# A decoder layer on one Trainium2 core: which queue loads the first projection weights, and how the convolution's state is loaded and turned

## The chip, the core and the metric

The kernel runs on one core of one Trainium2 chip. The core's engines work side by side, each through its own instructions in order: TensorE (PE in the profile; its weight loads are PEld), VectorE (DVE), ScalarE (ACT), GpSimd (POOL) and SyncE (SP), which here only issues transfers. ScalarE and GpSimd can issue transfers too. The metric is the device time of one execution in microseconds (us), the median of several runs.

## What is computed

One layer for a prompt of 1024 tokens and for 8 sequences of 8 new tokens, all in fp32. The reference, cut to what matters here:

```python
def layer_forward(h, p, pos, gla_s0, conv_prev, attend, lw):
    u = rmsnorm(h, lw['g_mix']) @ lw['w_in']
    ...                                  # gated linear attention -> o_gla, latent attention -> o_mla
    h = h + jnp.concatenate([o_gla, o_mla], axis=-1) @ lw['w_o']
    y, conv_new = conv_ffn(rmsnorm(h, lw['g_ffn']), conv_prev, lw)
    h = h + y
    h = h + (p @ lw['ple_w_proj']) * jax.nn.sigmoid(rmsnorm(h, lw['g_ple']) @ lw['ple_w_gate'])

def conv_ffn(n, prev, lw):
    a, c = n @ lw['ffn_w_gate'], n @ lw['ffn_w_up']
    full = jnp.concatenate([prev, a], axis=1)              # prev: state_conv, 2 rows per sequence
    conv = lw['ffn_conv_b'] + sum(lw['ffn_conv_w'][j] * full[:, j:j + T] for j in range(3))
    return (jax.nn.silu(conv) * c) @ lw['ffn_w_down'], full[:, -2:]
```

The model width is 1024, the inner width of the gated network 2816 (22 groups of 128). The new tokens attend to a paged cache of 8192 positions for each sequence.

## The kernel before

A float32 product is made of three matmuls. `split` writes an operand's rounded part with a cast (ScalarE, L115, names ending in h) and the remainder with a subtraction (VectorE or GpSimd, L116, names ending in l); a product is then high by high, high by low and low by high.

The longest stage streams the cache: for each block, pages are turned on TensorE (`ctp`, L522), split into `cTh` and `cTl`, multiplied into keys (`ks`, L139 to L141), squared and summed for the norm (`csq` on ScalarE, L560; `css` on VectorE, L565), scaled by `ca` and `cy` (L586 to L590), scored (`csr` from `kTh`, `kTl`; `sn`, L592 and L594 on GpSimd), reduced to a maximum (`ml`, L598), turned (`mt`, L616) and multiplied with the latents (`cpv`, L645, summed into `pvs`, L653). Beside it runs dense work for the prompt in small units that a generator hands out: from about 1060 us the output projection with w_o, `wo_units`. Each `wo_unit` is six matmuls into one PSUM bank, `ps_dn` (L1432, L1435, L1436), and one add on VectorE into the residual `h` (L1439). There are three groups of two row blocks c of w_o, each with two column halves f, and a fourth group for the end.

A projection operand is loaded into a buffer tagged "stage", of which there are three, and then split: `oraw` from the intermediate `doT` (`wo_rows`, L1409, into `sh`, `sl`) and `wraw` from w_o (`wo_cols`, L1417, into `wdh`, `wdl`). At the entry (g = 0, q = 0) SP issues, in the code's order, two oraw, two wraw for half 0, x blocks h0 to h3 (L1550, 128 x 1024 words each), two wraw for half 1, two oraw, h4 to h7 and `hs` (L1555). The first oraw and wraw blocks, up to `wraw_14736`, were loaded earlier.

At the end of the first group `conv_state` loads the convolution's weights (66 rows) and bias (22 rows) into the stage tile `cvec` (L1481, L1482), turns them on TensorE into `pt_cv` (L1484) and copies them to `convT` on ScalarE (L1486). Three more turns take 128, 128 and 96 rows of state_conv through stage tiles `sc` (L1492) and banks `pt_sc` (L1494) to `prev` (L1495). The banks pt_cv, pt_sc and ps_dn come from one pool of three. Another buffer in the same pool as the stage tiles, tagged "fd", is used by `fold_sample` (L1454 to L1456), which adds the new tokens' part of the projection into hs; between the first group's fold and the next there is a long pause.

In the last group each finished residual row block is taken up by `normed` (L1588): its squares are summed on ScalarE (L1465), its rows are stored as `dhp` by a transfer that ScalarE issues (L1592), and it is scaled in place, on VectorE in most cases (L1474). The scaling of a block in place waits for the landing of its store.

The order of each engine's instructions is not that of the code alone. The kernel is built inside a context that places instructions by a simulated timeline; the code's order and priorities are its input, and some matmuls are held where they stand. So a small edit can move other instructions.

## Time and profile before

| what | value |
|---|---|
| median of 3 runs | 2216.89 us (2215.88 to 2218.55) |
| the profiled execution | 2221.39 us |
| its span, first to last instruction | 2219.6 us |
| mean granted TensorE clock | 0.984 |
| TensorE busy | 2134.6 us (96%) |
| VectorE busy | 1666.6 us (75%) |
| ScalarE busy | 1369.1 us (62%) |
| GpSimd busy | 1227.5 us (55%) |

In the profile `L115` is line 115 of the kernel, `wdh<-wraw` means output from input without buffer numbers, and a bracket such as `[2.06 <-ACT wdh L115]` gives the idle time of the engine just before the instruction and what ended it. A group's time runs from the start of its first to the end of its last instruction. A window row gives each engine's busy time in a stretch, and the clock that TensorE was granted in it, 1.00 being full speed. The chain of waits follows the end of the program back through whatever released each step. PEq, SPq and ACTq are an engine's issuing of instructions and transfers.

### The profile page before, as it was taken

What the parts mean: (1) busy time and instruction counts of PE and PEld (TensorE: products, weight loads), DVE (VectorE), ACT (ScalarE), POOL (GpSimd) and SP (SyncE); (2) the same over time, 40 slices, a digit from 0 to 9 for tenths busy, and PEclk for the clock granted to TensorE, in tenths of its full rate; (3) what the DMA queues carried; (4) which work ended last, traced back from release to release, by engine and by line L of the source; (5) the groups of instructions that cost most, each with busy time, mean ns of one, the idle gap of its engine ahead of it and who ended that gap; (6) DMA issues with size and microseconds to landing.
All of it is one profiled execution on the core that took longest, in us unless ns stands there. A gap on an engine that the chain in (4) does not pass through costs nothing.

```text
span 2219.6 us, 38384 instructions
## 1 busy us (share of the span) xinstructions
PE 2134.6 (96%) x13460; PEld 1934.7 (87%) x13460; DVE 1666.6 (75%) x2551; ACT 1369.1 (62%) x3726; POOL 1227.5 (55%) x1330
## 2 busy tenths in 40 slices
PE   7999999999999999999999987999999999999999
PEld 6888978878888888887788876999999999888899
DVE  4775676467788888887888878888888886887642
ACT  5576766777778888887777766433333433534631
POOL 5675668576777777777445557666656562011100
PEclk9899999999999999999999998999999999999999
DMA  5343234412342222221521212322232325778321
GB/s 181 110 141 110 77 117 157 141 54 69 104 120 60 64 73 61 60 56 46 167 80 57 76 66 96 105 92 95 91 100 91 100 87 190 238 222 237 98 72 41
DMA packets 204418, 233.07 MB, mean 105 GB/s; under 512 B 42422, under 2 KB 146339, under 8 KB 204227
## 3 DMA queue, kind: packets, MB, share of 16 engines
q1 hardware_dynamic: 188259, 179.49, 25.8%
q0 software_dynamic: 14736, 46.67, 7.3%
q10 hardware_dynamic: 1232, 4.46, 0.5%
q8 instruction: 108, 1.77, 0.3%
q14 instruction: 83, 0.68, 0.1%
HBM read 188.00 MB, written 42.52 MB: 104 GB/s over the span
## 4 chain that ended last, share of the span: by engine, by line
PE 80%; DVE 7%; ACT 5%; DMA 4%; POOL 2%; issue 2%; SPq 0%; DVEq 0%; POOLq 0%; ACTq 0%
PE ps_gu L140 7%; PE ps_gu L141 7%; PE ps_gu L139 7%; PE ks L139 5%; PE ks L141 5%; PE ks L140 4%; PE ps_dn L141 3%; PE ps_dn L140 3%; PE ps_dn L139 3%; PE cpv L645 2%; PE ctp L522 2%; PE ps_lt L278 2%; PE ps_pj L139 2%; PE ps_pj L140 1%; PE ps_pj L141 1%
## 5 line engine op out<-in xcount | busy, mean ns | idle before, releaser
L560 ACT ACTIVATE csq<-ks 128x256 f32<-128x256 f32 x1040 | 392.2, 400 | 88.1 <-PE ks L141 78.0
L565 DVE TENSOR_REDUCE css<-csq 128x16 f32<-128x1024 f32 (+1 forms) x264 | 315.8, 1197 | 63.0 <-ACT csq L560 61.9
L115 ACT CAST wh<-st 128x512 fp32r<-128x512 f32 x176 | 108.4, 619 | 188.6 <-PE ps_gu L140 166.0
L139 PE MATMUL ks<-mv0h,cTh 128*128 128x320 f32 (+1 forms) x520 | 171.9, 333 | 6.9 <-ACT csq L560 3.0
L139 PE MATMUL ks<-mv1h,cTh 128*128 128x320 f32 (+1 forms) x520 | 170.4, 329 | 7.6 <-ACT sn L562 3.6
L604 POOL TENSOR_TENSOR chl<-craw,chl 128x1024 fp32r<-128x1024 f32 x64 | 141.8, 2216 | 57.9 <-ACT chl L603 57.2
L140 PE MATMUL ks<-mv1l,cTh 128*128 128x320 f32 (+1 forms) x520 | 154.0, 298 | 0.0
L140 PE MATMUL ks<-mv0l,cTh 128*128 128x320 f32 (+1 forms) x520 | 153.0, 296 | 0.0
L141 PE MATMUL ks<-mv0h,cTl 128*128 128x320 f32 (+1 forms) x520 | 148.6, 298 | 0.9 <-DVE cTl L116 0.8
L141 PE MATMUL ks<-mv1h,cTl 128*128 128x320 f32 (+1 forms) x520 | 148.9, 300 | 0.0
L630 POOL TENSOR_TENSOR phl<-sn,phl 128x512 fp32r<-128x512 f32 (+1 forms) x64 | 84.8, 1326 | 108.2 <-ACT phl L629 107.9
L116 DVE TENSOR_TENSOR wl<-st,wh 128x512 fp32r<-128x512 f32 x132 | 119.0, 903 | 28.5 <-ACT wh L115 28.5
L116 POOL TENSOR_TENSOR wl<-st,wh 128x512 fp32r<-128x512 f32 x44 | 69.4, 1580 | 103.5 <-ACT wh L115 98.2
L141 PE MATMUL ps_dn<-o 128*128 128x512 f32 x308 | 120.2, 390 | 0.0
L140 PE MATMUL ps_dn<-o 128*128 128x512 f32 x308 | 120.1, 390 | 0.1
L116 DVE TENSOR_TENSOR cTl<-ctp,cTh 128x512 fp32r<-128x512 f32 (+1 forms) x136 | 90.1, 663 | 39.4 <-ACT cTh L115 38.4
L139 PEld LDWEIGHTS ks<-mv0h,cTh 128*128 128x128 f32 x520 | 99.1, 191 | 20.7 <-ACT sn L562 7.1
L562 ACT COPY sn<-ks 128x64 f32<-128x64 f32 x520 | 116.8, 225 | 0.0
L139 PEld LDWEIGHTS ks<-mv1h,cTh 128*128 128x128 f32 x520 | 99.6, 191 | 19.7 <-ACT sn L562 7.4
L1317 POOL TENSOR_TENSOR pl<-p,ph 128x512 fp32r<-128x512 f32 (+1 forms) x96 | 97.1, 1016 | 31.7 <-DVE ph L1316 21.5
L139 PE MATMUL ps_dn<-o 128*128 128x512 f32 x308 | 112.1, 390 | 0.0
L139 PE MATMUL ps_gu<-xrh,wh 128*128 128x320 f32 x352 | 108.6, 309 | 1.1 <-ACT xrh L115 1.1
(672 smaller groups left out, 7875.3 us busy)
## 6 DMA issues: line engine op xcount, KB each, us to landing
raw<-ds SPq DMA_DIRECT2D x77, 256.0 KB
raw<-ffn_w_down SPq DMA_DIRECT2D x66, 256.0 KB
stage<-w_in SPq DMA_DIRECT2D x48, 256.0 KB
st<-ffn_w_gate SPq DMA_DIRECT2D x44, 256.0 KB
st<-ffn_w_up SPq DMA_DIRECT2D x44, 256.0 KB
wr<-ffn_w_down SPq DMA_DIRECT2D x44, 256.0 KB
ds<-cv SPq DMA_DIRECT2D x21, 512.0 KB
oraw<-doT SPq DMA_DIRECT2D x16, 256.0 KB
```

What stands on the lines that cost most here:

```text
L115: cast = act.copy(hi, src)
L116: res = (lo_eng or dve).tensor_tensor(lo, src, hi.bitcast(F32), ALU.subtract)
L139: pe.matmul(ps, ah, bh, start=first, stop=False)
L140: pe.matmul(ps, ah, bl, start=False, stop=False)
L141: return pe.matmul(ps, al, bh, start=False, stop=last)
L278: pe.matmul(ps, x, w, start=first, stop=last)
L560: act.activation(sq[:, f * 256:f * 256 + 256], ks[:, 0:256], AF.Square)
L562: act.copy(o.sn[:, g0 + i, :], ks[:, 256:320])
L565: dve.tensor_reduce(o.ss[:, g0 + i + 1 - n:g0 + i + 1, :].rearrange("p i h -> p (i h)"), sq2[:, :n].rearrange("p i (h n) -> p (i h) n", n= ...
L604: pool.tensor_tensor(ch[:, c0:c1, 128:256], src, ch[:, c0:c1, 0:128].bitcast(F32), ALU.subtract)
L630: pool.tensor_tensor(phl[:, :nt, 64:128], sb, phl[:, :nt, 0:64].bitcast(F32), ALU.subtract)
L1317: pool.tensor_tensor(pl[:, c0:], p[:, c0:], ph[:, c0:].bitcast(F32), ALU.subtract)
```

## The change

Two edits are made.

The first gives `wo_cols` an argument for the issuing queue. At the entry the first block of w_o for half 0 still goes through SP; the second block and both blocks of half 1 go through ScalarE's queue. The order in which the code names the loads stays the same.

The second loads everything that `conv_state` turns into one tile `cs` of 128 x 4 x 128 words in the "fd" buffer: three pieces of state_conv, and the convolution's weights and bias in the fourth column block. Four turns write 128, 128, 96 and 88 columns of one bank, and two copies on ScalarE take 352 columns to `prev` and 88 to `convT`, where there were four copies. The number of loads (five) and of turns (four) is as before.

```diff
-    def wo_cols(c, f):
+    def wo_cols(c, f, ring=sp):
...
-        sp.dma_start(raw, A["w_o"][0][c * P:(c + 1) * P, f * 512:f * 512 + 512])
+        ring.dma_start(raw, A["w_o"][0][c * P:(c + 1) * P, f * 512:f * 512 + 512])
...
     def conv_state():
-        cvec = stage([88, P], F32, "cvec")
-        sp.dma_start(cvec[0:66], A["ffn_conv_w"][0].rearrange("j (f p) -> (j f) p", p=P))
-        sp.dma_start(cvec[66:88], A["ffn_conv_b"][0].rearrange("(f p) -> f p", p=P))
+        cs = fold_tile([P, 4, P], F32, "cs")
+        scv = A["state_conv"][0].rearrange("b j (f p) -> (b j f) p", p=P)
+        parts = [(c, min(P, 352 - c * P)) for c in range(3)] + [(3, 88)]
+        for c, n in parts[:3]:
+            sp.dma_start(cs[:n, c], scv[c * P:c * P + n])
+        sp.dma_start(cs[0:66, 3], A["ffn_conv_w"][0].rearrange("j (f p) -> (j f) p", p=P))
+        sp.dma_start(cs[66:88, 3], A["ffn_conv_b"][0].rearrange("(f p) -> f p", p=P))
         pt = pd([P, 512], "pt_cv")
-        pe.transpose(pt[:, 0:88], cvec, ident[:88, :88])
+        for c, n in parts:
+            c0 = min(c * P, 352)
+            pe.transpose(pt[:, c0:c0 + n], cs[:n, c], ident[:n, :n])
         convT = z["convT"] = z["fx"].tile([P, 88], F32, name="convT")
-        act.copy(convT, pt[:, 0:88])
         prev = z["fx"].tile([P, 352], F32, name="prev")
-        scv = A["state_conv"][0].rearrange("b j (f p) -> (b j f) p", p=P)
-        for c0 in range(0, 352, P):
-            n = min(P, 352 - c0)
-            sc = stage([P, P], F32, "sc")
-            sp.dma_start(sc[:n], scv[c0:c0 + n])
-            pt = pd([P, 512], "pt_sc")
-            pe.transpose(pt[:, 0:n], sc[:n], ident[:n, :n])
-            act.copy(prev[:, c0:c0 + n], pt[:, 0:n])
+        act.copy(prev, pt[:, 0:352])
+        act.copy(convT, pt[:, 352:440])
...
-                    for ld, x in ((wo_rows, 0), (wo_cols, 0)):
-                        for c in grp:
-                            ld(c, x)
+                    for c in grp:
+                        wo_rows(c, 0)
+                    for c, ring in zip(grp, (sp, act)):
+                        wo_cols(c, 0, ring)
                     for t in range(NT):
                         sp.dma_start(hrows(t), A["x_prompt"][0, t * P:(t + 1) * P, :])
                         if t == 3:
-                            for ld, x in ((wo_cols, 1), (wo_rows, 1)):
-                                for c in grp:
-                                    ld(c, x)
+                            for c in grp:
+                                wo_cols(c, 1, act)
+                            for c in grp:
+                                wo_rows(c, 1)
```

The order of instructions differs from the entry of the projection (about 1060 us) to about 1282 us on all engines, is the same again to about 1318, and has small swaps from there to about 1390. The counts of matmuls are the same; ScalarE has two copies fewer and three transfers more, SP three transfers fewer.

At the entry, ScalarE's order (`-` before, `+` after; the number behind a name tells buffers apart) takes up the three transfers among the squares of one cache block:

```order
 L115 CAST cTh_15065<-ctp_15060 128x512
 L560 ACTIVATE csq_15011<-ks_15029 128x256
+L1417 DMA wraw_14742<-w_o 128x512
 L588 ACTIVATE ca_15047<-cy_15046 128x64
+L1417 DMA wraw_14752<-w_o 128x512
+L1417 DMA wraw_14758<-w_o 128x512
 L560 ACTIVATE csq_15080<-ks_15081 128x256
 L562 COPY sn_14985<-ks_15081 128x64
```

On SP, `wraw_14742` stood behind the fourth x block and the other two behind the fifth; now x blocks follow one another there. At the same place VectorE's order changes:

```order
 L565 TENSOR_REDUCE css_14986<-csq_15011 128x16
 L589 SCALAR_TENSOR_TENSOR ca_15047<-css_14802,ca_15047 128x64
+L590 SCALAR_TENSOR_TENSOR cy_15046<-ca_15047,cy_15046 128x64
 L565 TENSOR_REDUCE css_14986<-csq_15080 128x16
-L590 SCALAR_TENSOR_TENSOR cy_15046<-ca_15047,cy_15046 128x64
+L598 TENSOR_REDUCE ml_15055<-sn_14801 128x64
 L116 TENSOR_TENSOR wdl_14741<-wraw_14742,wdh_14740 128x512
-L598 TENSOR_REDUCE ml_15055<-sn_14801 128x64
+L622 TENSOR_SCALAR mt_15174,bm_15176<-mt_15174,bm_14965 128x128
 L1439 TENSOR_TENSOR h0_14699<-h0_14699,ps_dn_15104 128x512
```

The operation cy moved ahead of a css, and the maximum ml moved ahead of the remainder wdl of the second w_o block.

At the convolution's state, TensorE's order before, from the last keys of one block on:

```order
L141 MATMUL ks_16110<-mv0h_98,cTl_15846 128x256
L139 MATMUL csr_16216<-qbd0h_102,kTh_16212 128x256
L140 MATMUL csr_16216<-qbd0l_103,kTh_16212 128x256
L1484 MATMUL pt_cv_16143<-ident_61,cvec_16140 128x88
L141 MATMUL csr_16216<-qbd0h_102,kTl_16213 128x256
L139 MATMUL csr_16216<-qbd0h_102,kTh_16212 128x256
L140 MATMUL csr_16216<-qbd0l_103,kTh_16212 128x256
L141 MATMUL csr_16216<-qbd0h_102,kTl_16213 128x256
L1494 MATMUL pt_sc_16150<-ident_61,sc_16148 128x128
L1494 MATMUL pt_sc_16155<-ident_61,sc_16153 128x128
L1494 MATMUL pt_sc_16160<-ident_61,sc_16158 128x96
L1432 MATMUL ps_dn_16166<-wdh_15875,sh_15640 128x512
```

And after, the place to which the four turns moved:

```order
L1432 MATMUL ps_dn_16084<-wdh_14740,sh_14768 128x512
L1435 MATMUL ps_dn_16084<-wdl_14741,sh_14768 128x512
L1436 MATMUL ps_dn_16084<-wdh_14740,sl_14769 128x512
L1490 MATMUL pt_cv_16146<-ident_61,cs_16140 128x128 x2
L1490 MATMUL pt_cv_16146<-ident_61,cs_16140 128x96
L1490 MATMUL pt_cv_16146<-ident_61,cs_16140 128x88
L139 MATMUL ks_16093<-mv0h_98,cTh_15845 128x320
L140 MATMUL ks_16093<-mv0l_99,cTh_15845 128x320
```

The turns now stand a dozen units earlier, right behind the last ps_dn of a unit and ahead of the keys. The scores csr, which stood between the turns, follow only behind the next ps_dn (six matmuls), ctp (four) and two sets of ks (six). On ScalarE the copies to prev and convT moved ahead of the squares of this block, and the cast of `sh_16134` with the cast cTh after it. On SP the five loads stand ahead of two oraw and one wraw behind which they stood:

```order
 L1417 DMA wraw_16118<-w_o 128x512
+L1484 DMA cs_16140<-state_conv 128x128 x2
+L1484 DMA cs_16140<-state_conv 96x128
+L1485 DMA cs_16140<-ffn_conv_w 66x128
+L1486 DMA cs_16140<-ffn_conv_b 22x128
 L1409 DMA oraw_16124<-doT_84 128x512
 L1417 DMA wraw_16130<-w_o 128x512
 L1409 DMA oraw_16136<-doT_84 128x512
-L1481 DMA cvec_16140<-ffn_conv_w 66x128
-L1482 DMA cvec_16140<-ffn_conv_b 22x128
-L1492 DMA sc_16148<-state_conv 128x128
-L1492 DMA sc_16153<-state_conv 128x128
```

In the last group VectorE's scaling of h6 moved up. Before:

```order
L1439 TENSOR_TENSOR h6_14692<-h6_14692,ps_dn_18399 128x512
L1439 TENSOR_TENSOR h7_14693<-h7_14693,ps_dn_18415 128x512
L1439 TENSOR_TENSOR h7_14693<-h7_14693,ps_dn_18423 128x512
L653 SCALAR_TENSOR_TENSOR pvs_18448<-pvs_18291,mb_18397,cpv_18439 128x258
L1474 SCALAR_TENSOR_TENSOR h6_14692<-h6_14692,rs_14697,gb_14695 128x1024
L1439 TENSOR_TENSOR h0_14699<-h0_14699,ps_dn_18465 128x512
```

After:

```order
L1439 TENSOR_TENSOR h6_14692<-h6_14692,ps_dn_18391 128x512
L1439 TENSOR_TENSOR h7_14693<-h7_14693,ps_dn_18407 128x512
L1474 SCALAR_TENSOR_TENSOR h6_14692<-h6_14692,rs_14697,gb_14695 128x1024
L1439 TENSOR_TENSOR h7_14693<-h7_14693,ps_dn_18415 128x512
L653 SCALAR_TENSOR_TENSOR pvs_18440<-pvs_18283,mb_18389,cpv_18431 128x258
L1439 TENSOR_TENSOR h0_14699<-h0_14699,ps_dn_18457 128x512
```

The second add of h7 and pvs, which stood ahead of the scaling of h6, now stand behind it.

## The prediction

> **What bounds the kernel now.** I read the page first, then the chain of waits, then the windows of the two stretches that the change touches. The page gives the share of each engine in the chain that ended last:
>
> ```profile
> PE 80%; DVE 7%; ACT 5%; DMA 4%; POOL 2%; issue 2%; SPq 0%; DVEq 0%; POOLq 0%; ACTq 0%
> ```
>
> TensorE is the bound: 80% of the chain. So an edit is worth what it gives TensorE: idle time, or time at a lowered clock. The chain names both stretches by their transfers, w_o at the entry of the projection, then the convolution's loads (start, length, what):
>
> ```profile
> 1062.86 5.92 DMA wraw<-w_o
> ...
> 1069.46 1.32 DVE wdl L116
> ...
> 1145.13 1.90 DMA cvec<-ffn_conv_b
> ...
> 1151.01 0.43 PE ps_dn L1435
> ```
>
> The windows show what the second costs (columns: width, busy time of PE, PEld, DVE, ACT and POOL with counts, granted clock, DMA share, GB/s):
>
> ```profile
> 1144.00:1146.00 2.00, 1.26 (x11) 1.06 (x9) 1.73 (x4) 2.00 (x8) 0.81 (x1) 1.00 0.35 102
> 1146.00:1148.00 2.00, 1.34 (x8) 1.03 (x8) 1.73 (x2) 1.51 (x5) 1.98 (x2) 1.00 0.47 150
> 1148.00:1150.00 2.00, 0.47 (x2) 0.14 (x1) 2.00 (x4) 0.53 (x2) 0.57 (x2) 0.86 0.20 57
> 1150.00:1152.00 2.00, 1.86 (x5) 1.60 (x6) 0.33 (x1) 0.24 (x1) 1.76 (x2) 0.50 0.60 183
> 1152.00:1154.00 2.00, 2.00 (x8) 1.61 (x7) 0.69 (x1) 0.00 (x0) 1.78 (x2) 0.50 0.79 237
> 1154.00:1156.00 2.00, 2.00 (x10) 2.00 (x9) 1.34 (x2) 1.59 (x5) 0.00 (x0) 0.50 0.61 217
> 1156.00:1158.00 2.00, 2.00 (x11) 1.73 (x11) 1.19 (x2) 1.09 (x4) 0.23 (x1) 0.93 0.05 18
> 1160.00:1180.00 20.00, 20.00 (x130) 18.02 (x129) 15.34 (x23) 14.91 (x49) 8.84 (x8) 1.00 0.12 34
> ```
>
> Busy time by clock over the first seven rows is 1.26 + 1.34 + 0.40 + 0.93 + 1.00 + 1.00 + 1.86 = 7.8 us of work at full clock in 14 us: 6.2 us are lost, of which 3.1 are idle (14 less 10.93 busy) and 3.1 the half clock that follows. The last row says that a gain made here stays: behind it TensorE never waits for 20 us.
>
> By the Trainium skill, page "TensorE: Matmul & The Clock Gate", Part 1, the gate opens again after one busy window of about 3.4 us. Here the clock stays at 0.50 from 1150 to 1156 under unbroken work, over 6 us; by the page's window the half clock would cost about 1.7 us and not 3.1, and the sum below would be 1.4 us smaller. The measured rows decide.
>
> **The convolution's state: fewer waits.** The idle time has four pieces:
>
> ```profile
> 1146.29 0.39 PE L139 MATMUL csr<-qbd0h,kTh 128*128 128x256 f32 x1 [1.02 <-ACT kTh L115]
> 1147.16 0.27 PE L1484 MATMUL pt_cv<-ident,cvec 88*128 88x88 f32 x1 [0.37 <-DMA cvec<-ffn_conv_b]
> 1149.20 0.33 PE L1494 MATMUL pt_sc<-ident,sc 128*128 128x128 f32 x1 [1.06 <-DMA sc<-state_conv]
> 1150.14 0.39 PE L1494 MATMUL pt_sc<-ident,sc 96*128 96x96 f32 x1 [0.61 <-DMA sc<-state_conv]
> ```
>
> The last three are waits for loads, 2.04 us. The loads were late because their stage buffers were still held; the new tile takes the "fd" buffer, and SP has the five loads ahead of the next oraw. The last reader of that buffer ends here:
>
> ```profile
> 1115.83 0.67 DVE L1456 TENSOR_TENSOR hs<-hs,ps_ds 64x512 f32<-64x512 f32 x1
> ...
> 1146.75 0.62 ACT L115 CAST sh<-oraw 128x512 fp32r<-128x512 f32 x1
> 1148.18 0.27 ACT L1495 COPY prev<-pt_sc 128x128 f32<-128x128 f32 x1 [0.49 <-PE pt_sc L1494]
> 1154.04 0.58 ACT L115 CAST cTh<-ctp 128x512 fp32r<-128x512 f32 x1 [3.23 <-PE ctp L522]
> 1154.65 0.69 DVE L116 TENSOR_TENSOR cTl<-ctp,cTh 128x512 fp32r<-128x512 f32 x1 [0.78 <-ACT cTh L115]
> ```
>
> So the loads go out at about 1116.5, and with 1.90 us each they have long landed when their transposes come, near 1142. The five issues cost SP at most the same as before; no one waits for SP there. The 2.04 us go. The csr matmuls, for which kTh was awaited (1.02 us), now stand behind six ps_dn, four ctp and six ks matmuls, so that wait goes too.
>
> What is late next is ScalarE. It works without a gap up to 1147.4 (the end of the sh row), and still has the two new copies in front: the one of 352 columns I put at 0.45 us (0.27 for 128 columns in the row above, 0.62 for the 512 of sh; between these ends nearer the upper by its columns), the one of 88 as before, 0.23. Both stand ahead of sh now, so its end moves to about 1148.0, and the cast cTh after it ends at 1148.6. On VectorE sl (0.69, the length of cTl) stands ahead of cTl, which then ends at about 1149.6. TensorE has meanwhile run dry: it stood at about 1145.3 before the csr wait, has 0.44 us of transposes more by then, and then six ps_dn (0.43 at half clock in the chain, so 0.215 each, 1.3 in all) and ctp (0.4): about 1147.4. The first two ks need cTh alone (0.3 us), so it waits 1149.6 - 1147.4 - 0.3 = 1.9 us for the cast and the subtraction. The sum here is 6.2 - 1.9 = 4.3 us gained. The ends: 6.2, when nothing waits, and 2.04, when only the loads' waits go and the clock falls as before. VectorE would allow 5.0 (14 less its 9.0 us busy in the seven windows). Two copies fewer on ScalarE and no change in the transposes' columns: nothing more from these.
>
> **The entry's weights: ScalarE's queue.** Here TensorE stands from 1067.4 to 1070.8 but for one matmul:
>
> ```profile
> 1064.22 0.44 ACT L560 ACTIVATE csq<-ks 128x256 f32<-128x256 f32 x1
> 1066.30 1.22 DVE L565 TENSOR_REDUCE css<-csq 128x16 f32<-128x1024 f32 x1
> 1067.80 1.07 POOL L592 TENSOR_TENSOR sn<-sn,cy 128x512 f32<-128x512 f32 x1 [8.67 <-DVE cy L590]
> 1068.95 1.27 POOL L594 TENSOR_TENSOR sn<-sn,sr 128x512 f32<-128x512 f32 x1
> 1069.48 0.49 PE L1432 MATMUL ps_dn<-wdh,sh 128*128 128x512 f32 x1 [2.06 <-ACT wdh L115]
> 1070.69 1.04 DVE L598 TENSOR_REDUCE ml<-sn 128x64 f32<-128x512 f32 x1
> 1070.82 0.71 PE L1435 MATMUL ps_dn<-wdl,sh 128*128 128x512 f32 x1 [0.85 <-DVE wdl L116]
> ...
> 1068.00:1070.00 2.00, 0.49 (x1) 0.19 (x1) 0.54 (x1) 0.62 (x1) 1.92 (x2) 1.00 1.03 350
> 1070.00:1072.00 2.00, 1.18 (x3) 0.99 (x4) 1.74 (x3) 1.25 (x3) 0.42 (x2) 0.74 1.03 376
> 1072.00:1074.00 2.00, 2.00 (x10) 1.96 (x9) 1.89 (x3) 1.44 (x4) 0.04 (x1) 0.50 1.03 420
> ```
>
> The awaited block went out on SP at 1062.86, behind four x blocks, and landed at 1068.78. On ScalarE's queue it goes out behind the csq of 1064.22, so at about 1064.5, 1.6 us later. The DMA share is 1.03 with 350 to 420 GB/s: the engines are full, and moving the request makes no bytes fewer. If the two rings share the engines, a block of 256 KB has half of some 390 GB/s and takes 1.3 us, with the 1.90 us that the small cvec load took from issue to landing some 3.2 in all: it lands from 1067.7 on, and I allow up to 1068.8. If what was issued first is served first, it stands behind two more x blocks (h4 and h5, 128 x 1024 words each, 1.05 MB at 390 GB/s, 2.7 us) and lands at about 1071.5. I take the landing as unmoved, nearer the first.
>
> It then gives little, since VectorE's order changed: ml (L598) now stands ahead of the awaited wdl. The operation cy, for which POOL waits, is one place up and no longer stands behind the second css (1.22), so it is 1.2 us earlier: POOL's two operations end near 1069.0, ml near 1070.1, and wdl, 0.69 as the cTl of its size took, near 1070.9 instead of 1070.77 (1.32 in the chain's row, beside POOL). TensorE restarts at 1071.0 instead of 1070.8: +0.2 us. The ends: -3.0 (landing early, clock kept) and +2.7.
>
> **The drain.** At 1322 VectorE's order is changed in one more place, and with it some swaps up to 1365:
>
> ```profile
> 1318.76 1.87 DVE L1439 TENSOR_TENSOR h<-h,ps_dn 128x512 f32<-128x512 f32 x3
> 1320.98 0.33 ACTq L1592 DMA_DIRECT2D dhp<-h  x1
> 1322.25 1.29 DVE L1474 SCALAR_TENSOR_TENSOR h<-h,rs,gb 128x1024 f32<-128x1024 f32 x1 [0.97 <-DMA dhp<-h]
> 1340.00:1360.00 20.00, 14.06 (x80) 10.82 (x81) 18.57 (x27) 15.19 (x30) 17.98 (x15) 0.77 0.31 106
> ```
>
> The norm of h6 waits for the landing of dhp. It now stands ahead of the last of the three adds and of pvs, which wait with it: up to the 0.97 us on VectorE, which from 1340 on is the fullest engine (18.57 of 20). The swaps behind it may give as much back. I take 0, with ends of -1 and +1.
>
> The dhp row also prices **the three issues on ScalarE** at the entry: 0.33 us each, 1.0 in all; the csq behind them moves by up to that, inside the 2.06 us that TensorE waits there. Cover gone, it would cost the 1.0. SP, freed of three issues, sends h4 to h7 earlier; nobody waits for these.
>
> **The sum**: -4.3 + 0.2 + 0 = -4.1 us. The profiled execution is 2221.39 us (span 2219.6), 4.5 above the median of 2216.89; the sum is a difference, so from the median: 2212.8 us. A measurement here can tell 0.2%, 4.4 us, from no change, so the likeliest value lies just inside that.
>
> **Rivals.**
> 1. The clock falls again. The new wait of 1.9 us for cTh and cTl comes within a stretch already short of work. For it: at the entry 2.06 and 0.85 us of waiting were enough for 0.50. Against: 1.9 is a single, shorter gap. Half clock for 6 us costs the 3.1: -4.1 + 3.1 = -1.0, about 2215.9.
> 2. The entry gains: the rings share, the block lands at 1067.7 or before, ml does not hold wdl. TensorE's gap shrinks by some 2 us, and the loss by clock (0.31 + 1.00 us in the rows 1070 to 1074) mostly goes: -3 more, about 2209.6. The Trainium skill, "DMA: Bandwidth & Descriptors", section "Queues, rings and completion order", has each DMA engine alternate between rows of queues by packets, which is this rival; no run here shows it yet. The same page, "Issuing engines are not separate DMA queues", speaks against it: another issuing engine saves only the time to issue.
> 3. First come, first served: +2.7 at the entry instead of +0.2, about 2215.3.
> 4. Slower: ScalarE's blocks are served last, after all that SP has sent. Restart is landing plus 2.04 us (1070.82 less 1068.78), one for one. Eight x blocks (4.2 MB), and what follows, at 390 GB/s from 1061 reach to 1072 to 1076. With a landing at 1076.6 the restart is 7.8 later and the half clock, then 6 us long, costs some 1.7 more than now: 9.5 - 4.3 = +5.2, about 2222.1. The entry eats the conv place's gain from a landing near 1072 on, and past 1076 it is slower by over 0.2%.
> 5. It does not do what it says, the loads still late: excluded as far as row 1115.83 goes; only another wait of SP could hold them.
>
> **How the numbers follow.** Forecast 0.42, of which 0.24 falls below 2212.5; rival 1, 0.15; rival 2, 0.20; rival 3, 0.10; slower, rival 4 with reordered stretches (1160 to 1282) that open a wait like this one's, 0.13. Faster by over 0.2%: 0.24 + 0.20 = 0.44. Slower: 0.13. Same: 0.43. The range goes from the conv place's best end with the entry's (6.2 + 3.0 off, 2207.7) to the third rival with the drain's +1 and the conv place at its lower end (2215.3 + 1 + 2.3 = 2218.6). The forecast alone has 2211 to 2214.5.
>
> **What would show it.** Right: no DMA among what ends TensorE's waits at 1140 to 1160, the clock at 1.00 there, a wait for cTh or cTl of about 2 us, the loads into cs near 1116; at the entry wdh's cast still near 1068.8 and wdl behind ml. Wrong: a clock of 0.50 after 1149, a cast of wdh later than 1071 or before 1067.5, or a new gap of over 2 us between 1160 and 1282, where the order changed and I count nothing.

## The result, and the profile after

The changed kernel takes 2230.3 us in the median (2228.61 to 2233.31), the kernel before, run beside it, 2218.86. The ratio is 1.0056 with an interval of 1.0043 to 1.0068: 0.56% slower, where 2212.8 us were forecast. The profiled span grew from 2219.6 to 2228.9 us, by 9.3.

To see where, both traces were laid side by side at five marks that every kernel here has: the last transfer at line 1334 ahead of the projection (1059.16 us before), the 16th, 31st and 49th of VectorE's additions at L1439 (1142.85, 1216.31, 1313.02), and the 201st matmul into ps_gu (1408.00). The table is worked out from the start times of these instructions; each entry is what the stretch takes more than before, in us.

| kernel | ahead | entry, to the 16th add | convolution, to the 31st | to the 49th | drain, to ps_gu | difference of the spans |
|---|---|---|---|---|---|---|
| the change | +0.9 | **+8.1** | **-4.5** | 0.0 | **+4.8** | +9.3 |

So the convolution's place gained what was forecast, and both places that were put near zero lost. These are the windows of the entry, first of the changed kernel, then of the kernel before (width; busy time of PE, PEld, DVE, ACT and POOL with counts; granted clock, DMA share, GB/s):

```profile
1060.00:1080.00 20.00, 13.74 (x73) 10.91 (x71) 13.12 (x21) 11.55 (x38) 2.58 (x4) 0.91 0.95 307
1080.00:1100.00 20.00, 16.39 (x90) 14.20 (x91) 15.58 (x22) 12.59 (x41) 8.19 (x6) 0.91 0.30 101
```

```profile
1060.00:1080.00 20.00, 15.50 (x84) 13.02 (x84) 15.87 (x23) 14.96 (x49) 2.79 (x4) 0.91 1.01 339
1080.00:1100.00 20.00, 19.58 (x124) 17.07 (x123) 18.53 (x30) 14.22 (x47) 11.39 (x10) 1.00 0.22 70
```

TensorE idles 9.9 of the 40 us instead of 4.9, and the second window runs at 0.91 instead of 1.00, which is at most 1.8 us more. Most of the loss is idle time. The timeline of the changed kernel names its causes (start, length, instruction, and in brackets the idle time before it and what ended it):

```profile
1063.77 3.78 ACTq L1417 DMA_DIRECT2D wraw<-w_o  x1
1067.60 0.26 ACT L588 ACTIVATE ca<-cy 128x64 f32<-128x64 f32 x1 [2.05 <-issue]
1067.68 1.07 ACTq L1417 DMA_DIRECT2D wraw<-w_o  x2
1068.80 0.38 ACT L560 ACTIVATE csq<-ks 128x256 f32<-128x256 f32 x1 [0.94 <-DVE cy L590]
1069.34 0.41 PE L139 MATMUL ks<-mv0h,cTh 128*128 128x256 f32 x1 [3.02 <-ACT sn L562]
1073.39 0.62 ACT L115 CAST wdh<-wraw 128x512 fp32r<-128x512 f32 x1 [2.79 <-DMA wraw<-w_o]
1076.54 0.62 ACT L115 CAST wdh<-wraw 128x512 fp32r<-128x512 f32 x1 [2.04 <-DMA wraw<-w_o]
1094.13 0.38 PE L141 MATMUL csr<-qbd0h,kTl 128*128 128x256 f32 x1 [2.17 <-DVE kTl L116]
```

The first row is the surprise: to issue one 256-KB load holds ScalarE's queue for 3.78 us. What the engine had been given before still runs, but the activation ca behind the issue comes 2.05 us late (second row). Behind ca stand the two other issues, 1.07 us together (third), and only then the square csq (fourth) and the copy sn, for which TensorE waits 3.02 us (fifth). The awaited block is cast at 1073.39, 4.6 us after its old landing of 1068.78, or 3.7 us if the 0.9 us are taken off by which this execution was late ahead of the entry; ScalarE stands 2.79 us for it, and 2.04 for the next block (sixth and seventh). The last row is a later consequence, taken up at the end. A point for later: the second and third issues took 0.54 and 0.44 us, with 1.7 and 2.0 MB in flight on SP and the transfer engines as full (DMA share 1.00). Only the first was long.

At the convolution the windows of the changed kernel that answer to those of 1144 to 1158 before:

```profile
1152.00:1154.00 2.00, 1.69 (x14) 1.43 (x13) 2.00 (x3) 2.00 (x9) 1.10 (x1) 1.00 0.00 0
1154.00:1156.00 2.00, 2.00 (x15) 1.78 (x14) 1.44 (x4) 2.00 (x8) 1.09 (x2) 1.00 0.56 166
1156.00:1158.00 2.00, 2.00 (x17) 1.91 (x15) 2.00 (x1) 1.89 (x7) 2.00 (x1) 1.00 0.80 238
1158.00:1160.00 2.00, 1.72 (x12) 1.36 (x12) 2.00 (x5) 1.01 (x4) 0.77 (x2) 1.00 0.14 55
```

TensorE idles 0.6 us in eight, the clock stays at 1.00, and no load ends a wait. The loads' own rows and the waits that are left:

```profile
1124.16 1.28 SPq L1484 DMA_DIRECT2D cs<-state_conv  x3
1153.16 1.24 PE L645 MATMUL cpv<-chl,phl 128*128 128x258 f32 x8 [0.31 <-POOL phl L630]
1158.56 0.39 PE L141 MATMUL csr<-qbd0h,kTl 128*128 128x256 f32 x1 [0.28 <-DVE kTl L116]
```

In the drain the loss is made at two places. The first is where VectorE's order changed: the scaling of h6 now stands ahead of the second addition of h7. The changed kernel's rows, the scaling of h6, that addition, the store of h7 and the scaling of h7:

```profile
1326.83 1.28 DVE L1474 SCALAR_TENSOR_TENSOR h<-h,rs,gb 128x1024 f32<-128x1024 f32 x1 [0.44 <-DMA dhp<-h]
1328.03 0.68 DVE L1439 TENSOR_TENSOR h<-h,ps_dn 128x512 f32<-128x512 f32 x1
1328.85 0.33 ACTq L1593 DMA_DIRECT2D dhp<-h  x1
1332.54 1.28 DVE L1474 SCALAR_TENSOR_TENSOR h<-h,rs,gb 128x1024 f32<-128x1024 f32 x1 [0.88 <-POOL rs L1467]
```

Before, that addition was the last of the three at 1318.76, the store of h7 went out at 1320.98, and h7 was scaled here:

```profile
1324.92 1.76 DVE L1474 SCALAR_TENSOR_TENSOR h<-h,rs,gb 128x1024 f32<-128x1024 f32 x1
```

Counted from the start of the 49th addition, the store of h7 goes out after 11.3 us instead of 8.0, and h7 is scaled after 15.0 instead of 11.9. TensorE also runs at half clock there for 6.8 us (0.50 in 1320 to 1324), so that an addition waits 1.67 us for ps_dn; the two are not parted in this kernel. At VectorE's fifth scaling, the last but one, VectorE is 2.6 us behind (24.6 us after the 49th addition instead of 22.0).

The second place is the last scaling, that of h5, whose rows are here the last addition, the store and the scaling:

```profile
1349.02 0.67 DVE L1439 TENSOR_TENSOR h<-h,ps_dn 128x512 f32<-128x512 f32 x1
1349.83 0.33 ACTq L1593 DMA_DIRECT2D dhp<-h  x1
1353.71 2.40 DVE L1474 SCALAR_TENSOR_TENSOR h<-h,rs,gb 128x1024 f32<-128x1024 f32 x1 [1.58 <-DMA dhp<-h]
```

The kernel before had this at the same place:

```profile
1341.01 1.27 DVE L1439 TENSOR_TENSOR h<-h,ps_dn 128x512 f32<-128x512 f32 x2
1342.43 0.33 ACTq L1592 DMA_DIRECT2D dhp<-h  x1
1346.20 1.28 DVE L1474 SCALAR_TENSOR_TENSOR h<-h,rs,gb 128x1024 f32<-128x1024 f32 x1 [0.69 <-POOL rs L1467]
```

In both kernels the store goes out 0.14 to 0.15 us after the end of h5's last addition. That addition is 2.9 us late, and VectorE was 2.6 of them behind already. By the time VectorE came to scale h5 before, only POOL's rs was awaited; now the store is, for 1.58 us, and the scaling then takes 2.40 us and not 1.28, so that it ends 4.1 us late.

### The profile page after: what moved, and what is told of

Its sections match the earlier page's. It is cut to its first block, busy times and chain, and to the rows that moved or that the text cites. A ratio compares the mean times of both kernels' runs of the same rounds, so it can differ in the third digit from the quotient of the medians.

```text
span 2228.9 us, 38384 instructions
## 1 busy us (share of the span) xinstructions
PE 2137.7 (96%) x13460; PEld 1934.2 (87%) x13460; DVE 1671.7 (75%) x2551; ACT 1367.8 (61%) x3724; POOL 1228.8 (55%) x1330
## 4 chain that ended last, share of the span: by engine, by line
PE 44%; DVE 3%; POOL 2%; issue 1%; ACT 1%; DMA 1%; DVEq 0%; POOLq 0%; ACTq 0%
PE ps_gu L140 7%; PE ps_gu L141 7%; PE ps_gu L139 7%; PE ps_dn L141 3%; PE ps_dn L140 3%; PE ps_dn L139 3%; PE ps_pg L141 1%; PE ps_pg L140 1%; PE ps_pg L139 1%; PE ps_dn L1432 1%; PE ks L139 1%; PE ps_dn L1436 1%; PE ps_dn L1435 1%; PE ps_ds L1753 1%; PE ks L141 1%
## 5 line engine op out<-in xcount | busy, mean ns | idle before, releaser
L139 PE MATMUL ks<-mv0h,cTh 128*128 128x320 f32 (+1 forms) x520 | 171.7, 332 | 11.3 <-ACT sn L562 7.4
L592 POOL TENSOR_TENSOR sn<-sn,cy 128x512 f32<-128x512 f32 (+1 forms) x64 | 70.4, 1100 | 76.8 <-DVE cy L590 69.0
```

What stands on the lines that cost most here:

```text
L139: pe.matmul(ps, ah, bh, start=first, stop=False)
L592: pool.tensor_tensor(snv, snv, y[:, :nt].rearrange("p i h -> p (i h)").unsqueeze(2).broadcast_to([P, nt * 8, 8]), ALU.mult)
```

## The experiments

The kernels of one experiment differ from the change or from before by the lines shown. The table gives each one's median, the interval of its ratio to before (run beside it), and the stretches as above. The stretches are those of one profiled execution each, which need not be the median one: it lies 4.7 us below the median for the kernel with the convolution alone and the drain's order kept, 2.6 below for half 0, and 2.6 above for the last but one row.

| kernel | median us | ratio | ahead | entry | convolution | to the 49th | drain | spans |
|---|---|---|---|---|---|---|---|---|
| the change | 2230.30 | 1.0043 to 1.0068 | +0.9 | +8.1 | -4.5 | 0.0 | +4.8 | +9.3 |
| convolution alone | 2218.16 | 0.9981 to 1.0002 | -2.5 | -1.0 | -5.4 | 0.0 | +5.5 | -3.2 |
| ring alone | 2231.58 | 1.0044 to 1.0073 | +0.8 | +8.8 | +0.1 | 0.0 | +0.4 | +10.0 |
| half 0 on ScalarE | 2225.26 | 1.0013 to 1.0034 | -0.6 | +3.8 | -5.4 | -1.6 | +4.7 | +1.2 |
| half 1 on ScalarE | 2225.39 | 1.0016 to 1.0037 | -0.6 | +4.9 | -4.4 | 0.0 | +4.0 | +3.8 |
| weights first | 2219.13 | 0.9984 to 1.0006 | -1.4 | -0.8 | -5.4 | +0.1 | +4.1 | -2.3 |
| the same, half 0 on ScalarE | 2226.95 | 1.0012 to 1.0036 | +1.5 | +5.0 | -5.4 | -1.4 | +5.6 | +5.5 |
| convolution alone, drain's order kept | 2214.06 | 0.9961 to 0.9987 | -4.0 | -1.3 | -5.4 | -1.6 | +0.3 | -12.0 |
| x in halves | 2219.65 (one time) | | -1.8 | +0.2 | -5.4 | -1.3 | +5.3 | -1.9 |
| weights alone first | 2212.54 | 0.9958 to 0.9983 | -1.1 | -2.9 | -5.4 | +0.2 | +0.1 | -9.1 |
| the same, half 0 on ScalarE | 2214.82 | 0.9968 to 0.9988 | -1.6 | +0.9 | -5.4 | -0.3 | +2.5 | -4.0 |
| the change, drain's order kept | 2224.92 | 1.0009 to 1.0035 | +0.8 | +7.5 | -4.4 | 0.0 | +0.2 | +4.1 |

Ahead of the first mark all kernels are alike, so the +1.5 to -4.0 us there are how much one execution differs from another. Two kernels have before's order at the entry too, and read -1.0 and -1.3 there: so far single executions can be off. "Half 0" is the one block of the first half that the change moves to ScalarE, "half 1" the other two.

**Convolution alone.** From the change, with before's code at the entry.

```diff
-                    for c in grp:
-                        wo_rows(c, 0)
-                    for c, ring in zip(grp, (sp, act)):
-                        wo_cols(c, 0, ring)
+                    for ld, x in ((wo_rows, 0), (wo_cols, 0)):
+                        for c in grp:
+                            ld(c, x)
```

> Only the convolution's tile, all w_o blocks through SP. Every engine has the order of before up to the convolution and that of the change from there on. Theory A (the loss is made at the entry by ScalarE's queue, the convolution's place gives its 4.4 us, the drain's extra 4.7 us is an accident of the clock): no loss at the entry, -4 us in all, about 2214.5 us. Theory B (the new order at the drain costs 4.7 us in itself): -4.4 + 4.7, no change, about 2219. In both TensorE waits for no load between 1140 and 1160 us.

The convolution gives 5.4, and the drain takes 5.5 back: the ratio cannot be told from 1. The entry has nothing to do with the drain's loss. Nor does that loss need the half clock, for here TensorE's clock is 1.00 from 1304 to 1345, and what h6 costs stands by itself (its scaling, then the store of h7):

```profile
1313.36 2.99 DVE L1474 SCALAR_TENSOR_TENSOR h<-h,rs,gb 128x1024 f32<-128x1024 f32 x1 [2.22 <-DMA dhp<-h]
1317.09 0.33 ACTq L1591 DMA_DIRECT2D dhp<-h  x1
```

VectorE stands 2.22 us for the store of h6, where it stood 0.97 before, and the scaling takes 2.99 us instead of 1.29. The second addition of h7 is behind it, so the store of h7 goes out 13.0 us after the 49th addition instead of 8.0, and at the fifth scaling VectorE is 3.0 us behind.

**Ring alone.** From the change, with before's convolution code.

```diff
-        cs = fold_tile([P, 4, P], F32, "cs")
...
+        cvec = stage([88, P], F32, "cvec")
...
```

> Only ScalarE's queue at the entry, the convolution as before. Order of the change at the entry, of before from the convolution on. Theory A: the entry loses 8 us as in the change, nothing comes back, about 2227 us, and the convolution's place again loses about 6 us of TensorE's work. Rival (the entry's loss is an accident of one run): an entry loss that differs from 8 us by over 3 us.

The entry costs 8.8 by itself and the drain nothing: the two losses belong to the two parts of the change. ScalarE's queue again, in this kernel's timeline:

```profile
1063.63 4.02 ACTq L1417 DMA_DIRECT2D wraw<-w_o  x1
1067.71 0.26 ACT L588 ACTIVATE ca<-cy 128x64 f32<-128x64 f32 x1 [2.29 <-issue]
```

**Half 0 on ScalarE, half 1 on ScalarE.** From the change, one or the other block put back on SP.

```diff
-                                wo_cols(c, 1, act)
+                                wo_cols(c, 1)
```

> As the change, but only the second block of half 0 goes through ScalarE, both blocks of half 1 through SP as before. Theory H (ScalarE is held in order by the issue of that one block, which takes 3.8 us instead of 0.33 while SP's x blocks fill the DMA engines): the issue is again over 3 us long, ca is late by over 2 us, TensorE waits about 3 us for sn or csq near 1066 us; entry +3 to +5 us. Theory L (the loss comes from late landings on ScalarE's ring): no such wait, but the block lands 4 us later than on SP; entry +2 to +4 us. The blocks of half 1 land as before in both. Total with the convolution's -4.4: -1 to +1 us against before.

```diff
-                    for c, ring in zip(grp, (sp, act)):
+                    for c, ring in zip(grp, (sp, sp)):
```

> As the change, but the second block of half 0 goes through SP, only the two blocks of half 1 through ScalarE. All engines but ScalarE's and SP's queues have the order of the change. Theory H: without the first issue ScalarE isn't held before ca, so cy comes 1 to 2 us earlier than in the change; the next issue may be held in its place, ahead of csq. Theory L: the half 1 blocks land 8 us after their issue as in the change (11 us), the stop near 1081 to 1086 us stays; entry +4 us. Total with the convolution's -4.4: 0 us against before, or +4 where both apply.

The first costs 3.8 at the entry, the second 4.9, both together 8.1: either block does about half of the harm. The second kernel has the change's order of work on every engine; only that one transfer is on another queue. In both the first issue on ScalarE is long and the block lands late; these are the first kernel's rows, then the second's:

```profile
1062.26 3.69 ACTq L1417 DMA_DIRECT2D wraw<-w_o  x1
1065.99 0.26 ACT L588 ACTIVATE ca<-cy 128x64 f32<-128x64 f32 x1 [1.95 <-issue]
1072.83 0.62 ACT L115 CAST wdh<-wraw 128x512 fp32r<-128x512 f32 x1 [4.84 <-DMA wraw<-w_o]
```

```profile
1062.83 2.89 ACTq L1417 DMA_DIRECT2D wraw<-w_o  x1
1065.81 0.38 ACTq L1417 DMA_DIRECT2D wraw<-w_o  x1
1066.24 0.38 ACT L560 ACTIVATE csq<-ks 128x256 f32<-128x256 f32 x1 [2.08 <-DVE cy L590]
1071.68 0.62 ACT L115 CAST wdh<-wraw 128x512 fp32r<-128x512 f32 x1 [2.52 <-DMA wraw<-w_o]
```

In the second kernel the square behind the two issues starts 0.05 us after the second issue ends, though its bracket names cy. The second issue is short again, 0.38 us, with 2.4 MB in flight on SP.

**Weights first, and the same with half 0 on ScalarE.** If it is the x blocks in flight that hold the issue and delay the block, the block on SP ahead of all x should be early, and on ScalarE, with nothing ahead of it, harmless. The x blocks are pinned behind the weights. The second kernel has `(sp, act)` where the diff has `(sp, sp)`.

```diff
-                    for c, ring in zip(grp, (sp, act)):
+                    for c, ring in zip(grp, (sp, sp)):
                         wo_cols(c, 0, ring)
+                    for c in grp:
+                        wo_cols(c, 1)
                     for t in range(NT):
-                        sp.dma_start(hrows(t), A["x_prompt"][0, t * P:(t + 1) * P, :])
-                        ...
+                        tc.keep_in_program_order(sp.dma_start(hrows(t), A["x_prompt"][0, t * P:(t + 1) * P, :]))
+                    for c in grp:
+                        wo_rows(c, 1)
```

> The convolution's tile as in the change; at the entry all w_o blocks go through SP and the x blocks are held behind them on SP. Theory (what TensorE waits for at the entry is w_o behind 2 MB of x): the awaited block goes out near 1062.9 us with free DMA engines, lands within 3 us, TensorE's two waits of 2.06 and 0.85 us and the half clock behind them go: entry -3 to -4 us, convolution -4.4, the drain's order is nearly that of before (h6 scaled behind pvs): 0 to +2. In all -6 us, ratio 0.997. Rival (the x blocks and what stands behind them are now late by 2 us and are waited for instead): entry 0 or above, ratio 0.999 or above.

> As e5, but the second block of half 0 goes through ScalarE, while no x block is in flight. Theory (ScalarE's issue is held and its block late because SP's x blocks fill the DMA engines): issue 0.3 to 0.6 us, landing within 3.5 us of it, no wait of ScalarE ahead of ca; the entry within 1 us of e5's. Rival (an issue on ScalarE in the middle of its work, or the first use of its ring, is slow by itself): issue 2.9 us or more again, entry +3 to +4 us against e5.

Neither was the test it was meant to be: the loads of hs, gb and WvT (1.0 MB), which were not pinned, floated ahead of the weights on SP. The first kernel gained nothing at the entry (-0.8, as much as kernels whose entry is before's), although the awaited block was cast 2.5 us earlier, counted from the first mark: an early block by itself was no gain here. The second lost 5.0 with an issue of 2.76 us. When that issue began, no x block was in flight, but SP sent three of them while it lasted, so the two kernels do not clear the x blocks.

**Convolution alone, the drain's order kept.** The norm of h6 is pinned behind the second addition of h7, where it stood before; for h6, normed leaves the scaling to the pinned line.

```diff
                 if f:
-                    normed(t)
+                    if t == 7:
+                        tc.keep_in_program_order(dve.scalar_tensor_tensor(hrows(6), hrows(6), z["rs"][:, 6:7], z["gb"], ALU.mult, ALU.mult))
+                    normed(t, t == 6)
```

> Only the convolution's tile, as in the run with it alone, but in the last group the scaling of h6 is held behind the second add of h7, so that the engines' order there is that of before but for one row. Theory (the drain's +3 to +5.5 us of all kernels with the new tile comes from the order there): drain within 1 us of before, total -5 us, ratio 0.9975. Rival (it comes from where the clock's windows fall): drain +3 us or more again, ratio 0.999.

The drain's +5.5 becomes +0.3 and the kernel is 0.13% to 0.39% faster than before. The store of h7 goes out 8.0 us after the 49th addition, as before. The rows of its timeline at h5 read as before's did, the store right behind two additions, and VectorE waiting for POOL's rs alone:

```profile
1328.80 1.26 DVE L1439 TENSOR_TENSOR h<-h,ps_dn 128x512 f32<-128x512 f32 x2
1330.21 0.33 ACTq L1593 DMA_DIRECT2D dhp<-h  x1
1333.98 1.28 DVE L1474 SCALAR_TENSOR_TENSOR h<-h,rs,gb 128x1024 f32<-128x1024 f32 x1 [0.69 <-POOL rs L1467]
```

**x in halves.** The change, with each x block loaded in two halves of 512 columns, so that its rows are as long as those of w_o (2048 bytes and not 4096).

```diff
-                        sp.dma_start(hrows(t), A["x_prompt"][0, t * P:(t + 1) * P, :])
+                        for e in range(2):
+                            sp.dma_start(hrows(t)[:, e * 512:e * 512 + 512], A["x_prompt"][0, t * P:(t + 1) * P, e * 512:e * 512 + 512])
```

> As the change, but each x block is loaded in two halves, in rows of 2048 bytes like those of w_o instead of 4096. Theory (the two rings take turns packet by packet): while both are busy ScalarE's ring moves as many bytes as SP's, near 190 KB per us instead of the 136 of the change, and its first block needs 1.4 us from first to last byte instead of 2. If the hold of ScalarE's issue goes by the number of packets ahead of it, it grows from 3.8 toward 6 us; if by bytes, it stays.

Neither expectation is what came. The entry's loss almost went (+0.2), more than an equal share could give: of the bytes moved in the 2 us after the first, ScalarE's ring had 516 of 688 KB. The issue is shorter, and the cast 6.1 us earlier than in the change, of which 2.7 are by how much this execution was ahead at the first mark:

```profile
1061.09 1.97 ACTq L1417 DMA_DIRECT2D wraw<-w_o  x1
1067.28 0.62 ACT L115 CAST wdh<-wraw 128x512 fp32r<-128x512 f32 x1 [2.06 <-DMA wraw<-w_o]
```

SP had 1.0 MB in flight at that issue and not 2.5. So this kernel changed two things, the share and what was ahead, and cannot part them; why ScalarE's ring got three packets for each of SP's is open.

**Weights alone first, with half 0 on SP or on ScalarE.** As the pair above, but the loads of hs, gb and WvT are pinned behind x too, each in this way. Nothing is pinned in the drain; VectorE's order there came out as before's up to the scaling of h5.

```diff
-                    sp.dma_start(z["hs"], A["x_sample"].rearrange("b t d -> (b t) d"))
+                    tc.keep_in_program_order(sp.dma_start(z["hs"], A["x_sample"].rearrange("b t d -> (b t) d")))
...
```

> As e5, but x_sample, g_ffn and WvT, which stood ahead of w_o in e5, are held behind the x blocks too, so that w_o has the DMA engines to itself; the drain has TensorE's order of before. Theory (w_o behind other transfers is what TensorE waits for at the entry): block issued near 1062.9 as counted in before, landed 2.5 us later, TensorE's gaps at the entry under 1 us in all, entry -3 us; convolution -4.4, drain 0: -7 us, ratio 0.9967. Rival (VectorE and POOL give TensorE its other waits there, and the x blocks come late): entry -1 as in e1 and e7, ratio 0.9975.

> As e9, but the second block of half 0 goes through ScalarE with nothing but w_o in flight. Theory (ScalarE's issue is held, and its bytes start, only when what SP had in flight is through): issue under 1 us, first bytes within 3 us of the start of the issue, ca not late by over 0.7 us; entry within 1 us of e9's. Rival (an issue on ScalarE is slow by itself): issue over 2.5 us again and entry +3 to +4 us against e9.

On SP the entry gains 2.9 and the kernel is the fastest here: 2212.54 us, 0.17% to 0.42% faster than before (the interval overlaps that of the kernel with only the drain kept). Its windows at the entry:

```profile
1060.00:1080.00 20.00, 16.72 (x102) 13.96 (x101) 19.08 (x27) 15.10 (x52) 6.01 (x6) 1.00 0.83 297
1080.00:1100.00 20.00, 19.73 (x127) 17.36 (x125) 15.66 (x27) 15.66 (x49) 10.69 (x11) 1.00 0.21 66
```

TensorE idles 3.6 of the 40 us and never loses its clock. Of the 2.9 us, 1.7 are the piece of half clock that before's trace has at the entry; the kernel with the drain kept, whose entry is before's, has none there either, so this part need not come from the new order. The two kernels' issue and cast, SP first, ScalarE second:

```profile
1061.76 1.53 SPq L1417 DMA_DIRECT2D wraw<-w_o  x3
1064.58 0.62 ACT L115 CAST wdh<-wraw 128x512 fp32r<-128x512 f32 x1 [0.22 <-DMA wraw<-w_o]
```

```profile
1061.25 1.10 ACTq L1417 DMA_DIRECT2D wraw<-w_o  x1
1062.87 0.31 ACT L588 ACTIVATE ca<-cy 128x64 f32<-128x64 f32 x1
1066.05 0.62 ACT L115 CAST wdh<-wraw 128x512 fp32r<-128x512 f32 x1 [2.21 <-DMA wraw<-w_o]
```

With nothing in flight the hold is gone as expected (1.10 us, and ca waits for no issue). But the block is cast 1.5 us later than on SP, though issued no later, and ScalarE waits 2.21 us for it: its first bytes come after 2.6 us, and while it moves, SP's queue moves 372 KB, of which 312 are the two w_o blocks of half 1 and 60 of x, which on SP's own queue stand behind it. That, with the half clock that follows, is 3.8 us at the entry of these two executions, which I had not expected. The medians are only 2.3 us apart, and the two intervals overlap, so what ScalarE's queue costs here is not clear of noise. The drain's +2.5 with before's order there is not explained by an order: the trace has two pieces of half clock more (at 1309.7 and 1340.4, 3.4 us each). Why they fall there is open.

**The change, the drain's order kept.** The whole change with the pin of the drain.

> The whole change, with the scaling of h6 held behind the second add of h7 as in e7. If the parts add up (entry +8, convolution -4.4, drain 0 instead of +4.7): +3.5 us against before, ratio 1.0016, and -5 us against the change. If the drain's loss depends on when it is reached: ratio 1.004 or more.

+7.5 at the entry, -4.4 at the convolution, +0.2 in the drain, slower than before by 0.09% to 0.35%. The parts add up: the drain's order is worth 4.6 us (4.8 less 0.2), and what is left of the loss is the ring's.

## Why the prediction was wrong

**"The sum here is 6.2 - 1.9 = 4.3 us gained": right.** Measured 4.5 in the change, and 5.4 in the kernels that left ScalarE's queue alone, gave it one block, or had x in halves. That the loads' waits and the half clock would go was seen rightly; that the sum is met so closely is luck, for the reason given for the 1.9 was wrong: no wait of that size for cTh or cTl came. What was left at the place was 0.31 for phl and 0.28 for kTl, which the kernels with 5.4 do not have, and TensorE was given work throughout. The loads went out at 1124 and not near 1116, since SP had other issues before them; they were still early enough. Rival 1, the clock falling again, did not come.

**"I take the landing as unmoved, nearer the first" and "0.33 us each, 1.0 in all": the entry failed, +8.1 instead of +0.2.** Both terms failed at the same thing, ScalarE's first issue while SP had 2.5 MB in flight.

The issue was priced from the dhp row, where the engines had little to do. Here the first held the queue 3.78 us and not 0.33; the other two took 0.54 and 0.44. The prediction set what is behind it inside TensorE's wait of 2.06 us for the block; a wait of 3.02 us for sn opened ahead of that one instead.

The block came 4.6 us later (3.7 from the first mark), and the cast at 1073.39 is the sign of being wrong that the prediction named, one later than 1071. Counted from the packets in the traces, for the first issue on ScalarE of each kernel:

| kernel | issue, us | KB in flight on SP | us to the first bytes | KB that SP moved meanwhile | packets in the next 2 us, ScalarE's ring and SP's | KB, the same |
|---|---|---|---|---|---|---|
| the change | 3.78 | 2468 | 6.9 | 2496 | 125 and 130 | 250 and 520 |
| ring alone | 4.02 | 2540 | 7.2 | 2896 | 129 and 134 | 258 and 536 |
| half 0 on ScalarE | 3.69 | 2052 | 7.3 | 2628 | 114 and 150 | 228 and 556 |
| half 1 on ScalarE | 2.89 | 2056 | 6.0 | 2404 | 130 and 130 | 260 and 520 |
| weights first, half 0 on ScalarE | 2.76 | 592 | 5.9 | 1684 | 103 and 126 | 206 and 504 |
| x in halves | 1.97 | 988 | 4.4 | 1164 | 258 and 86 | 516 and 172 |
| weights alone first, half 0 on ScalarE | 1.10 | 0 | 2.6 | 176 | 128 and 171 | 256 and 372 |
| the change, drain's order kept | 3.78 | 2604 | 6.6 | 2584 | 130 and 135 | 260 and 540 |

In the change the block waits until what SP had in flight is through (6.9 us, 2496 KB); in the other kernels SP moves about as much as it had in flight, or up to 1.1 MB more, before the block's first bytes. Only then do the rings take turns, and in four of the eight kernels nearly packet by packet. An x packet has 4096 bytes and one of w_o 2048, so ScalarE's ring has a third of the bytes. The prediction reckoned with a half, from the first moment. So rival 3 ("First come, first served: +2.7") was right about the wait and too small in size, for it counted two x blocks ahead where there were 2.5 MB; rival 4 named the place of the loss and its price for a late block, but with the block at 1073 rather than 1076, and without the hold.

The Trainium skill, "DMA: Bandwidth & Descriptors", "Queues, rings and completion order", has the engines alternate between queues by packets. The 125 and 130 packets agree with it once both rings are being served; the 258 and 86 of x in halves do not, and the 6.9 us before that are not in what it says. The same page's "Issuing engines are not separate DMA queues" has it that issuing on several engines saves only issue time, usually small; here it cost some, 3.78 us on the engine in TensorE's chain.

How far the hold and the late landing each go into the 8.1 is not parted. Half 0 has both and costs 3.8; half 1 has both and costs 4.9. With an issue of 1.10 us and no wait behind it, the block on ScalarE is still 3.8 us worse than the same block on SP (+0.9 against -2.9), in one execution of each. The changed order of VectorE at the entry was not tried with all loads on SP; in the change's trace ml is done at 1072.8, ahead of the cast that wdl waits for, so it did not hold wdl.

**"I take 0, with ends of -1 and +1": the drain failed, +4.8.** The place was right and its price was not. The prediction counted that the second addition of h7 and pvs wait with the scaling of h6, up to 0.97 us, and that the swaps behind may give it back. It left out what hangs on that addition: the store of h7, its landing and the scaling of h7, which came 3.1 us later. VectorE was 2.6 us behind at the fifth scaling in the change, and 3.0 in the convolution alone, where the wait itself had grown to 2.22 us and the scaling to 2.99. At h5, where no wait for a store stood before, the store is awaited too, 1.58 us. Holding h6's scaling behind h7's second addition took the loss away (+0.3 and +0.2 in two kernels), so the order is its cause. The half clock of the drain in the change (6.8 us from 1318.7) was not foreseen either, and why the scalings grew to 2.99 and 2.40 us was not tried.

**The sum.** 0.9 + 8.1 - 4.5 + 4.8 = 9.3, the difference of the spans. Of the four numbers only the third was seen.

## What to carry to other kernels

The first issue on a queue, made while another has megabytes in flight, cannot be priced from an issue made when little moves (0.33 us against 3.78 here), nor from the issues that follow it (0.35 to 0.54); and an issue that sits in the queue of an engine others wait for is work on their path. Nor is a second ring a way past what the first has in flight. A block that is awaited is brought forward by putting it ahead of the bulk on the same queue, and the order pinned, since small loads slip in ahead; what it gains in time is another matter, for beside the kernel with only the drain kept the gain here is not clear of noise. After any edit under a scheduler, the places far from the edit where the order moved must be read for an addition that moved behind a wait, and for the store and the scaling that hang on it: their price was as large here as the edit's gain.

## What the runs showed of the hardware

**An issue can hold its engine's queue for microseconds.** 3.78 us with 2.5 MB in flight on the other queue, 1.10 with none, 0.33 in the drain. It does not follow what is in flight in step: 1.97 us with 988 KB, but 2.76 with 592, of which 256 were in packets of 256 bytes. And it was only ever the first issue on ScalarE's queue: those behind it took 0.35 to 0.54 us with 0.7 to 2.4 MB in flight on SP. SP's queue has such an issue too, 2.87 us in the kernel before at 1071.10 with 2.3 MB in flight. The first use of ScalarE's queue alone is not it, for in the kernel before that is a store at 1319.47, of 0.36 us. What holds the issue is open.

**A VectorE subtraction grew from 0.7 to 4.0 us beside GpSimd.** The wait of 2.17 us for kTl at 1094.13 has its origin here; the changed kernel's timeline of VectorE and GpSimd, then before's, then that of the kernel with the weights alone first:

```profile
1089.73 4.01 DVE L116 TENSOR_TENSOR sl<-oraw,sh 128x512 fp32r<-128x512 f32 x1 [1.11 <-ACT sh L115]
1089.61 1.44 POOL L594 TENSOR_TENSOR sn<-sn,sr 128x576 f32<-128x576 f32 x1
1090.99 2.19 POOL L604 TENSOR_TENSOR chl<-craw,chl 128x1024 fp32r<-128x1024 f32 x1
```

```profile
1083.04 1.75 DVE L116 TENSOR_TENSOR sl<-oraw,sh 128x512 fp32r<-128x512 f32 x1
1082.82 1.43 POOL L594 TENSOR_TENSOR sn<-sn,sr 128x576 f32<-128x576 f32 x1
```

```profile
1081.15 0.69 DVE L116 TENSOR_TENSOR sl<-oraw,sh 128x512 fp32r<-128x512 f32 x1 [1.24 <-ACT sh L115]
```

The subtraction ends some 0.5 us after GpSimd's operations do: beside two that follow at once 4.01 us, beside one 1.75, beside none of this kind 0.69. That it is GpSimd that holds it was not tried by itself. The Trainium skill, "GPSIMD Engine Reference", section "Specifications", says that the two engines share their access to the memory when VectorE has two operands there; the rows agree.

**Half clock comes in pieces of about 3.4 us.** In the clock records of all traces here its stretches are 3.4, 6.8, 10.2 or 13.7 us long, but for the one that runs into each trace's end. So a short gap can cost one piece or three: the wait of 3.02 us for sn stands beside one piece in the change (from 1069.6), that of 3.03 us in the ring alone beside three (from 1067.4). The two pieces that the prediction read as over 6 us of half clock under unbroken work run from 1149.5 to 1156.3 in the kernel before; the first still holds the end of the wait of 0.61 us before 1150.14, so only the second was unbroken work. The stretch to the 49th addition, with equal code, is 1.6 us shorter in the kernel with the convolution alone and the drain's order kept, whose clock in 1210 to 1315 is 1.00, where it is 0.98 before: about what half clock for one such piece takes.
